# Two-layer decoder step, mixer: the beginning reordered, the turned rows of x kept in DRAM, the bias rows copied per pair of heads from SBUF

## The chip, the cores and the metric

The kernel runs on one core of one Trainium2 chip. The core has a matrix engine (TensorE, "PE" in the profile, with its weight loads as "PEld"), a vector engine (VectorE, "DVE"), a scalar engine (ScalarE, "ACT"), a general one (GpSimd, "POOL") and a small one that here only issues DMAs (SyncE, "SP"). DMAs are carried out by 16 DMA engines that all issuing engines share. The metric is the time of one execution in microseconds (us) on the device.

## The reference: what is computed

The program is one inference step of a hybrid decoder layer on 544 tokens, 512 of a prompt and 32 of a sample group (8 sequences of 4 tokens), with a model width of 1024. All numbers are fp32.

```
h = RMSNorm_pre(x)
[x_r | q | k | v | g] = h @ W_in
A: x_r -> causal conv of width 4 -> RG-LRU (gates, scan)
B: attention over a window of 128, 8 query heads, 2 key/value heads,
   a sink per head, a bias by relative position (rel_bias by bucket)
m = (sigmoid(g_A) * (A @ W_lru_o) + sigmoid(g_B) * (B @ W_attn_o)) @ W_out
x = x + RMSNorm_post(m)
u = RMSNorm_pre2(x) @ W_up ; causal conv of width 3
x = x + RMSNorm_post2((gelu(u_gate) * u_val) @ W_down)
```

The outputs are the new x of both groups, the states of the LRU and of both convolutions, and the key and value caches. In the bias, the score of query i and key j gets `rel_bias[bucket(i - j), head]`, and minus infinity outside the window.

## The kernel before, in words

**Products.** An fp32 product is made of three: each operand is split into a high part (fp32r) and the rest, and hi·hi, hi·lo and lo·hi are added up in PSUM. A weight block of 1024 x 128 (512 KB, a "key") is loaded by SP into one of five raw buffers (`wload`, L254) and split in two units of four 128x128 blocks: `wsplit_hi` on ACT (L277) and `wsplit_lo` on DVE (L282). One `step` (L331) multiplies a key with one half of the tokens (columns 0 to 255 or 256 to 543; in the later projections 272 and 272), which is 8 chunks x 3 = 24 matmuls into one PSUM tile (`pmin` for W_in, `pmlo` for W_lru_o, `pmout` for W_out).

**Order.** PE, ACT and DVE run exactly in the order of the program text. After each step a `tick` (L194) issues the other work: first the high splits of the weights that are claimed, two keys ahead, then whatever generators are due (`start_at(t, ...)` puts one on the list from tick t on; each `yield` ends its share of a tick), then the evacuations of the step before (`late`), then the low splits, and at the end what is in `last`. In the kernel before, the instructions of POOL and SP are put in order by the framework's planner, in the kernel after those of SP alone. An engine waits for semaphores in its own order: an instruction that waits holds up everything behind it on that engine. A DMA waits on the engine that issues it, and is then carried out by the DMA engines.

**The beginning.** SP loads x of the first two token blocks (four halves of 256 KB in all), a few norm rows, then weights and the rest of x. PE runs 36 matmuls on constants (WARM = 18 in the text, each of them two passes), then turns the 8 norm rows (`ps_rows_a`, L386). The mean square is taken on ACT and DVE, x is scaled by 1/rms (L423, L425), and PE turns x into 8 chunks of 128 channels x 256 tokens (`ps_ta`, L448). From each, ACT writes the high part of h, multiplied by the norm weight (`hH`, L433) and DVE the low part (`hL`). Then the first product runs: 8 hi·hi matmuls, 8 with the low weights, 8 with hL. In ticks 1 and 2 the same is done for the other 288 tokens (`norm_b`, `ps_tb` L461), for the steps from the fifth on.

**Bias tables.** `attn_tables` (L545 on) starts at tick 2. One matmul pair (`ps_ohp`) gives 8 rows (one per head) of 384 bias values by distance. DVE copies them to SBUF (`rvec`, L549), POOL stores them to DRAM (`rscr`, L550, 12 KB) and then repeats each row 128 times with one DMA from DRAM to DRAM (`rrep`, L553, 1536 KB). From `rrep` the table of a pair of heads, 128 x 2 x 256, is loaded with a row shift of one element per query (`btab`, L581), at ticks 5, 11, 18 and 27. The first softmax of a head pair adds it to the scores (`s` <- `psc`, `btab` on DVE, L177).

**Sample tables.** `sample_tables` starts at tick 12. POOL copies 16 small blocks of `rel4` into `lt` (L559), loads a one-hot matrix `ohs` (L561) and two masks `mk` (L565), and PE multiplies `ohs` and `lt` (`ps_bs`). The product stands in PE's order between two steps of W_in, so PE does nothing else until `ohs` and `lt` are there.

**x again.** At the product with W_lru_o (16 steps of `pmlo`) x is needed unscaled and turned, as `x1`, for the residual sum after W_out. `x_again` (L995) loads the five token blocks anew into the raw buffers (`xx`, L998), PE turns them (`pxx`, L1004, 40 transposes in 10 groups), and ACT and DVE copy them into `x1` (L1008). In the same stage POOL adds the gated halves (`gl`, L1019, one 128x272 per step) and issues the stores of the LRU states (L907 to L910).

## Time and profile before

| | before |
|---|---|
| median of 3 runs | 1002.67 us (1002.42 to 1002.88) |
| profiled execution: its time | 1003.73 us |
| profiled execution: its span | 1002.0 us |
| TensorE clock granted, mean | 0.997 |
| PE busy | 988.9 us (99%) |
| DVE busy | 732.0 us (73%) |
| ACT busy | 579.4 us (58%) |
| POOL busy | 151.0 us (15%) |
| DMA: mean over the span | 133 GB/s |

The profile is of one execution; times inside it are counted from the start of the span. In a row of the timeline stand the start, the duration, the engine, the line of the kernel, the operation, and the tile that is written <- the tiles that are read, then the number of instructions that were put together in the row; what stands in square brackets is the time that the engine was idle before it and what it waited for. An engine name with a q behind it is its instruction queue, which issues DMAs. In a row of the windows stand, for a stretch of time, the busy time of PE, PEld, DVE, ACT and POOL (with the number of instructions), the clock that TensorE was granted (1.00 is full), the busy share of the 16 DMA engines and the GB/s moved. In the list of DMA issues stand the number, the KB of each and the median time from the issue to the landing.

### The profile page before, as it was taken

How to read it: one execution, taken by the hardware profiler on the slowest of the kernel's cores; microseconds unless marked ns; L12 is line 12 of the kernel's file. 1: busy time of each engine (PE TensorE's matmuls, PEld its weight loads, DVE VectorE, ACT ScalarE, POOL GpSimd, SP SyncE). 2: the span in 40 equal slices, each digit the busy share in tenths (PEclk: the TensorE clock that was granted, in tenths of full speed). 3: DMA queues.
4: the chain of work that ended last, by engine and by line, in shares of the span. 5: the costliest groups of instructions: out<-in, count | busy, mean ns of one | idle time of the engine just before them, and what ended most of it. 6: DMA issues, size and time to landing. Idle time of an engine off the chain costs nothing.

```text
span 1002.0 us, 20195 instructions
## 1 busy us (share of the span) xinstructions
PE 988.9 (99%) x7837; PEld 978.5 (98%) x7837; DVE 732.0 (73%) x1555; ACT 579.4 (58%) x1422; POOL 151.0 (15%) x270
## 2 busy tenths in 40 slices
PE   8999999999999999999999999999999999999997
PEld 7999999999999999999999999999999999999996
DVE  6476687545846555589777788888888888887865
ACT  6444455469358535456776756565656565656652
POOL 3131010002304432110001111111111111110004
PEclk9999999999999999999999999999999999999999
DMA  7743223333322345327245858586867676767712
GB/s 211 231 150 93 64 77 105 99 91 94 102 68 85 106 138 148 105 66 210 71 116 124 193 124 192 125 191 127 189 133 184 139 177 145 171 160 167 216 45 90
DMA packets 207687, 133.40 MB, mean 133 GB/s; under 512 B 6546, under 2 KB 194306, under 8 KB 207560
## 3 DMA queue, kind: packets, MB, share of 16 engines
q1 hardware_dynamic: 197944, 112.20, 39.4%
q0 software_dynamic: 9600, 17.90, 11.3%
q10 hardware_dynamic: 48, 2.03, 0.5%
q8 instruction: 61, 1.00, 0.4%
q14 instruction: 34, 0.28, 0.1%
HBM read 111.82 MB, written 9.14 MB: 121 GB/s over the span
## 4 chain that ended last, share of the span: by engine, by line
PE 92%; DVE 3%; ACT 2%; DMA 2%; issue 0%; SPq 0%; ACTq 0%; DVEq 0%
PE pmin L165 22%; PE pmdn L165 16%; PE pux L1400 15%; PE puy L1400 7%; PE pq L1400 6%; PE pmout L165 5%; PE pmao L165 5%; PE pmlo L165 4%; PE puz L1400 4%; PE pg L165 1%; PE psc L165 1%; PE pvp L165 1%; DMA raw_up_s<-in_w_up_dram 1%; DMA raw_in<-in_w_in_dram 1%; PE pt L701 1%; PE ptok L165 1%
## 5 line engine op out<-in xcount | busy, mean ns | idle before, releaser
L165 PE MATMUL pmin<-hH,wh_in 128*128 128x256 f32 (+1 forms) x576 | 167.8, 294 | 0.0
L165 PE MATMUL pmin<-hH,wl_in 128*128 128x256 f32 (+1 forms) x576 | 164.7, 288 | 0.0
L165 PE MATMUL pmin<-hL,wh_in 128*128 128x256 f32 (+1 forms) x576 | 164.6, 288 | 0.0
L165 PE MATMUL pmdn<-fH,wh_dn 128*128 128x256 f32 (+1 forms) x448 | 129.2, 288 | 0.2 <-DVE ft L174 0.2
L165 PE MATMUL pmdn<-fH,wl_dn 128*128 128x256 f32 (+1 forms) x448 | 129.2, 288 | 0.2 <-DVE wl_dn L168 0.2
L165 PE MATMUL pmdn<-fL,wh_dn 128*128 128x256 f32 (+1 forms) x448 | 129.1, 288 | 0.0
L177 DVE SCALAR_TENSOR_TENSOR uc<-u,fv,uc 128x560 f32<-128x560 f32 x128 | 102.0, 797 | 13.3 <-ACT uc L1431 13.2
L165 PEld LDWEIGHTS pmin<-hH,wh_in 128*128 128x128 f32 x576 | 108.9, 190 | 1.9 <-issue 1.2
L165 PEld LDWEIGHTS pmin<-hL,wh_in 128*128 128x128 f32 x576 | 108.1, 188 | 0.0
L165 PEld LDWEIGHTS pmin<-hH,wl_in 128*128 128x128 f32 x576 | 107.9, 188 | 0.0
L165 PEld LDWEIGHTS pmdn<-fH,wh_dn 128*128 128x128 f32 x448 | 84.5, 189 | 0.6 <-issue 0.6
L165 PEld LDWEIGHTS pmdn<-fH,wl_dn 128*128 128x128 f32 x448 | 84.4, 188 | 0.4 <-DVE wl_dn L168 0.4
L165 PEld LDWEIGHTS pmdn<-fL,wh_dn 128*128 128x128 f32 x448 | 84.3, 188 | 0.0
L1526 ACT COPY u<-pux 128x272 f32<-128x272 f32 x52 | 20.1, 387 | 86.1 <-PE pux L1400 86.1
L168 DVE TENSOR_TENSOR u<-puy,u 128x240 f32<-128x240 f32 (+2 forms) x78 | 24.6, 344 | 49.8 <-PE puy L1400 32.1
L174 DVE TENSOR_TENSOR ft<-ft,pmdn 128x256 f32<-128x256 f32 (+1 forms) x104 | 45.2, 436 | 16.7 <-PE pmdn L165 16.1
L277 ACT ACTIVATE wh_in<-raw_in 128x512 fp32r<-128x512 f32 x72 | 44.2, 629 | 19.3 <-PE pmin L165 8.4
L282 DVE TENSOR_TENSOR wl_in<-raw_in,wh_in 128x512 fp32r<-128x512 f32 x72 | 48.2, 683 | 0.8 <-ACT wh_in L277 0.8
L1431 ACT ACTIVATE uc<-u,fv 128x560 f32<-128x560 f32 x64 | 48.2, 754 | 0.0
L664 ACT ACTIVATE s<-s,st 128x256 f32<-128x256 f32 (+1 forms) x32 | 15.2, 475 | 50.4 <-DVE st L661 43.0
L168 DVE TENSOR_TENSOR wl_dn<-raw_dn,wh_dn 128x512 fp32r<-128x512 f32 x56 | 38.3, 684 | 0.0
L1326 POOL DMA_DIRECT2D raw_up_s<-raw_up_s x26 | 22.7, 874 | 102.9 <-issue 5.2
(776 smaller groups left out, 3404.3 us busy)
## 6 DMA issues: line engine op xcount, KB each, us to landing
raw_in<-in_w_in_dram SPq DMA_DIRECT2D x36, 512.0 KB
raw_dn<-in_w_down_dram SPq DMA_DIRECT2D x56, 256.0 KB
raw_up_s<-in_w_up_dram SPq DMA_DIRECT2D x26, 512.0 KB
raw_up_s<-raw_up_s POOLq DMA_DIRECT2D x26, 256.0 KB, 5.9
raw_ao<-in_w_attn_o_dram SPq DMA_DIRECT2D x8, 512.0 KB
raw_lo<-in_w_lru_o_dram SPq DMA_DIRECT2D x8, 512.0 KB
raw_out<-in_w_out_dram SPq DMA_DIRECT2D x8, 512.0 KB
x1d<-x SPq DMA_DIRECT2D x8, 272.0 KB
```

Of the source, the lines that this page charges most:

```text
L165: pe.matmul(out, l, r, start=start, stop=stop)
L168: dve.tensor_tensor(out=out, in0=a, in1=b, op=ALU.subtract)
L174: dve.tensor_tensor(out=out, in0=a, in1=b, op=ALU.add)
L177: dve.scalar_tensor_tensor(out=out, in0=a, scalar=s_, in1=b, op0=op0, op1=op1)
L277: act.activation(hl[0], raw, AF.Copy)
L282: (eng or dve).tensor_tensor(out=hl[1], in0=raw, in1=f32(hl[0]), op=ALU.subtract)
L664: act.activation(s3[:, j, :], s3[:, j, :], AF.Exp, bias=ng[:, j:j + 1], accum_out=sm[:, j:j + 1])
L701: pe.transpose(pt[:, (2 * ch + j) * P:(2 * ch + j + 1) * P], s3[:, j, ch * P:(ch + 1) * P], ident)
L1326: pool.dma_start(out=w["p4"], in_=w["p2"], accum_op=ALU.add)
L1400: pe.matmul(ps[:, :HN], w, x, start=start and k == 0 and i == 0, stop=stop and k == 3 and i == 2, skip_group_check=True)
L1431: act.activation(yt[j][:, 0:FLATU], u[:, 0:FLATU], AF.Copy, scale=fv[:, j:j + 1])
L1526: act.copy(e[nm_], z)
```

## The change

The beginning of the mixer is written anew:

- Loads. The norm rows `rows_a` are loaded between the two first blocks of x. `relx`, `ohp`, the other norm rows and `rel4` are loaded on SP's queue, no longer on POOL's; the weights 3 and 4 come behind the first of them. 12 warming passes (24 matmuls) stand ahead of the turning of the norm rows and 11 (22 matmuls) behind it.
- First product. The low splits of the first key go to POOL. The transposes of two chunks share a PSUM tile (four tiles `ps_ta0` to `ps_ta3`), and the first product is spread between the transposes: the hi·hi and hi·lo matmuls of a chunk come as soon as its parts are written, the 8 with low weights at the end.
- The turned rows of x are kept: `keep_a` copies the 8 chunks of 256 tokens from PSUM to eight SBUF slots `xn` (four on ACT, four on DVE, at the ends of ticks 1 and 2), `keep_b` the 8 of 288 tokens. At tick 6 `put_away` takes the reciprocal of 1/rms and stores it and the 8 slots (272 KB each) to DRAM (`rmsd`, `xdram`).
- `x_again` loads the 8 chunks into `x1` and a row of rms repeated over all partitions, and POOL multiplies each chunk (128x544) by it, one per tick. No loads of `xx`, no transposes, no copies.
- Bias rows. `rvec` is no longer stored to DRAM and repeated with one DMA for all 8 rows. For each pair of heads `load_rep` issues one DMA on POOL that reads the pair's two rows of `rvec` in SBUF, each 128 times, and writes `rrep` of that pair (384 KB) to DRAM; `load_btab` then loads the table as before. The four copies are due at ticks 4, 5, 12 and 20, the tables at 4, 9, 17 and 26.
- POOL's instructions run in the order of the text too, with those of PE, ACT and DVE. In that order stand, after the first splits: copy 0, table 0, copy 1, table 1, the stores `kout` and `vout` of the first key/value head, copy 2, the 16 copies into `lt`, `ohs`, `mk`, the 23 small instructions of the gate constants (`lz` to `cc`), table 2, and later copy 3 and table 3.

```diff
@@ -72,7 +72,8 @@
 FIRST = 5
 ATTN = (8, 10, 12, 14, 16, 18, 20, 22, 24, 27, 30, 33, 36, 39, 42, 45)
 SAMPLE = (41, 46)
-WARM = 18
+WARM = 12
+KEEP = 11
 GATES = (51, 53, 55, 57, 73, 74, 75, 76)
 EXPS = (58, 59, 60, 61, 78, 79, 80, 81)
 SCANS = (62, 63, 65, 67, 82, 83, 85, 86)
@@ -138,7 +139,7 @@
     ctx.enter_context(tc.manual_schedule(engines={pe.engine}))
     mixer = ExitStack()
     cp = mixer.enter_context(tc.tile_pool(name="mixer_const", bufs=1))
-    mixer.enter_context(tc.manual_schedule(engines={act.engine, dve.engine}))
+    mixer.enter_context(tc.manual_schedule(engines={act.engine, dve.engine, pool.engine}))
 
     def S(name, dt=F32):
         return sp.tile([P, SLOT], dt, tag="s", name=name)
@@ -314,13 +315,6 @@
 
     def mmhalf(ps, key, X, a, ks=range(KD)):
         n = X.half[a][1] - X.half[a][0]
-        if key == order[0] and a == 0:
-
-            for j, (i0, i1) in enumerate(((0, 0), (1, 0), (0, 1))):
-                for k in ks:
-                    mm(ps[:, :n], wunits[2 * wpos[key] + k // 4][i0][:, k % 4, :], X.get(k, a, i1),
-                       j == 0 and k == 0, j == 2 and k == KD - 1)
-            return
         for k in ks:
             wh, wl = (wunits[2 * wpos[key] + k // 4][j][:, k % 4, :] for j in range(2))
             xh, xl = X.get(k, a, 0), X.get(k, a, 1)
@@ -330,9 +324,11 @@
 
     def step(key, X, a, done, target=None, look=2, quick=False):
 
-
-        ps = PM("pm" + "_".join(str(z) for z in key) + f"_{a}")
-        if quick:
+        first_ = key == order[0] and a == 0
+        ps = first_ps if first_ else PM("pm" + "_".join(str(z) for z in key) + f"_{a}")
+        if first_:
+            pass
+        elif quick:
             mmhalf(ps, key, X, a, range(4))
             now[0] += 0.5
             sides()
@@ -361,22 +357,23 @@
             nc.sync.dma_start(out=xt[i, z][:n, 0:512], in_=src[:, 512 * z:512 * z + 512])
 
     xload(0)
+    nc.sync.dma_start(out=rows_a[0:8, :], in_=I["norm_mix_pre"].rearrange("o (k p) -> (o k) p", p=P))
     xload(1)
-    nc.sync.dma_start(out=rows_a[0:8, :], in_=I["norm_mix_pre"].rearrange("o (k p) -> (o k) p", p=P))
     wload(0)
     wload(1)
     xload(2)
     xload(3)
     xload(4)
-    for i in (2, 3, 4):
-        wload(i)
+    wload(2)
     relx = cp.tile([NBK + 1, NH], F32, name="relx")
     pool.memset(relx, 1.0)
-    pool.dma_start(out=relx[0:NBK, :], in_=I["rel_bias"])
+    nc.sync.dma_start(out=relx[0:NBK, :], in_=I["rel_bias"])
     ohp = T("ohp")[:NBK + 1, 0:3 * WIN]
-    pool.dma_start(out=ohp, in_=I["c_ohp"])
+    nc.sync.dma_start(out=ohp, in_=I["c_ohp"])
     for r, nme in ((8, "norm_mix_post"), (16, "norm_ffn_pre"), (24, "norm_ffn_post")):
-        pool.dma_start(out=rows_a[r:r + 8, :], in_=I[nme].rearrange("o (k p) -> (o k) p", p=P))
+        nc.sync.dma_start(out=rows_a[r:r + 8, :], in_=I[nme].rearrange("o (k p) -> (o k) p", p=P))
+    wload(3)
+    wload(4)
     pv = keep.tile([P, 96], F32, name="pv")
 
     pw = PX("ps_warm")
@@ -384,6 +381,8 @@
     for z in range(WARM):
         mm(pw[:, (z % 4) * P:(z % 4 + 1) * P], ones, ident, True, True)
     pe.transpose(ps0[:, 0:8], rows_a[0:8, :], ident[0:8, 0:8])
+    for z in range(KEEP):
+        mm(pw[:, (z % 4) * P:(z % 4 + 1) * P], ones, ident, True, True)
     G_PRE, G_POST, G_FPRE, G_FPOST, C_W, C_B, C_BR, C_BI, C_LAM = 0, 8, 16, 24, 32, 64, 72, 80, 88
 
     def newton_rstd(r, v, s_, sq):
@@ -435,22 +434,63 @@
 
     xsquares(0)
     xsquares(1)
+    act.copy(pv[:, 0:8], ps0[:, 0:8])
     xrstd(0, 2)
-    split = [wsplit_hi(u) for u in wclaim(2)]
-    xscale(0, "av")
-    xscale(1, "vv")
-    dve.tensor_copy(pv[:, 0:8], ps0[:, 0:8])
-    for u in split:
-        wsplit_lo(*u)
+    u0, u1 = wclaim(2)
+
+    def scale0(i, z):
+        dve.tensor_scalar(xt[i, z][:, 0:512], xt[i, z][:, 0:512], ss[:, 1, i:i + 1], None, ALU.mult)
+
+    scale0(0, 0)
+    scale0(1, 0)
+    act.activation(xt[1, 1][:, 0:512], xt[1, 1][:, 0:512], AF.Copy, scale=ss[:, 1, 1:2])
+    scale0(0, 1)
+    first_ps = PM("pm_first")
+
+    def first_mm(k, i0, i1, start=False, stop=False):
+        mm(first_ps[:, :256], wunits[k // 4][i0][:, k % 4, :], h.get(k, 0, i1), start, stop)
+
+    ps_ta = []
+    wsplit_lo(*wsplit_hi(u0), eng=pool)
+    for k in range(KD + 3):
+        if k < KD:
+            if k % 2 == 0:
+                ps_ta.append(PX(f"ps_ta{k // 2}"))
+                for z in range(4):
+                    pe.transpose(ps_ta[-1][:, z * P:(z + 1) * P], xtile(z % 2, k + z // 2), ident)
+            hsplit(k, 0, ps_ta[-1][:, k % 2 * 256:k % 2 * 256 + 256])
+        if k == 1:
+            wsplit_lo(*wsplit_hi(u1), eng=pool)
+        if 0 <= k - 2 < KD:
+            first_mm(k - 2, 0, 0, start=k == 2)
+        if 0 <= k - 3 < KD:
+            first_mm(k - 3, 0, 1)
     for k in range(KD):
-        ps = (PM if k in (5, 6) else PX)(f"ps_ta{k}")
-        for i in range(2):
-            pe.transpose(ps[:, i * P:(i + 1) * P], xtile(i, k), ident)
-        hsplit(k, 0, ps[:, :256])
+        first_mm(k, 1, 0, stop=k == KD - 1)
+
+    xn = [S(f"xn{k}") for k in range(KD)]
+    xdram = drp.tile([KD, P, NT], F32, name="xdram")
+    rms = cp.tile([P, 5], F32, name="rms")
+    rmsd = drp.tile([5, P], F32, name="rmsd")
+
+    def keep_a(k):
+        (dve.tensor_copy if k % 2 else act.copy)(xn[k][:, 0:256], ps_ta[k // 2][:, k % 2 * 256:k % 2 * 256 + 256])
+
+    def keep_b(k, ps):
+        (act.copy if k % 2 else dve.tensor_copy)(xn[k][:, 256:NT], ps[:, :288])
+
+    def put_away():
+        dve.reciprocal(rms, ss[:, 1, :])
+        nc.sync.dma_start(out=rmsd.rearrange("i p -> p i"), in_=rms)
+        for k in range(KD):
+            nc.sync.dma_start(out=xdram[k], in_=xn[k][:, 0:NT])
+        yield
 
     def norm_b():
         last.extend(lambda i=i: xsquares(i) for i in (2, 3, 4))
-        yield
+        last.extend(lambda k=k: keep_a(k) for k in range(4))
+        yield
+        last.extend(lambda k=k: keep_a(k) for k in range(4, KD))
         last.append(lambda: xrstd(2, 5))
         last.extend(lambda i=i, e=e: xscale(i, e) for i, e in ((2, "av"), (3, "av"), (4, "vv")))
         yield
@@ -459,7 +499,7 @@
             for i in (2, 3, 4):
                 t0, n, _ = TOK[i]
                 pe.transpose(ps[:, t0 - 256:t0 - 256 + n], xtile(i, k), ident[:n, :n])
-            late.append(lambda k=k, ps=ps: hsplit(k, 1, ps[:, :288]))
+            late.append(lambda k=k, ps=ps: (hsplit(k, 1, ps[:, :288]), keep_b(k, ps)))
             if k in (3,):
                 yield
 
@@ -535,22 +575,17 @@
     pool.memset(lt, 0.0)
     rel4 = cp.tile([P, NH], F32, name="rel4")
     for t in range(DT):
-        pool.dma_start(out=rel4[32 * t:32 * t + 32, :], in_=I["rel_bias"])
+        nc.sync.dma_start(out=rel4[32 * t:32 * t + 32, :], in_=I["rel_bias"])
     biasS = cp.tile([P, 2, SKEY], F32, name="biasS")
-    rscr = drp.tile([NH, 3 * WIN], F32, name="rscr")
-    rrep = drp.tile([NH, P, 3 * WIN], F32, name="rrep")
+    rvec = cp.tile([NH, 3 * WIN], F32, name="rvec")
+    rrep = [drp.tile([2, P, 3 * WIN], F32, name=f"rrep{hp}") for hp in range(4)]
     btab = {}
 
     def attn_tables():
         ps = PX("ps_ohp")
         mm(ps[:NH, 0:3 * WIN], relx, ohp, True, True)
         yield
-        rvec = T("rvec")[:NH, 0:3 * WIN]
         dve.tensor_copy(rvec, ps[:NH, 0:3 * WIN])
-        pool.dma_start(out=rscr, in_=rvec)
-
-        a = rscr[:, :]
-        pool.dma_start(out=rrep, in_=bass.AP(a.tensor, a.offset, [[3 * WIN, NH], [0, P], [1, 3 * WIN]]))
         yield
 
     def sample_tables():
@@ -574,9 +609,13 @@
             add(biasS[:, g, :], ps[:, 0:SKEY], mk[g])
         yield
 
+    def load_rep(hp):
+        r = rvec[2 * hp:2 * hp + 2, :]
+        pool.dma_start(out=rrep[hp], in_=bass.AP(r.tensor, r.offset, [list(r.ap[0]), [0, P], [1, 3 * WIN]]))
+
     def load_btab(hp):
         bt = S(f"btab{hp}")[:, 0:512].rearrange("p (h j) -> p h j", h=2)
-        src = rrep[2 * hp:2 * hp + 2, :, :]
+        src = rrep[hp][:, :, :]
         a = bass.AP(src.tensor, src.offset + WIN - 1, [[3 * WIN - 1, P], [3 * WIN * P, 2], [1, 2 * WIN]])
         pool.dma_start(out=bt, in_=a)
         btab[hp] = bt
@@ -916,11 +955,13 @@
         yield
 
     start_at(1, norm_b())
+    start_at(6, put_away())
     start_at(2, attn_tables())
     start_at(9, params())
     start_at(14, cache_shift())
     for hp in range(4):
-        start_at((5, 11, 18, 27)[hp], once(load_btab, hp))
+        start_at((4, 5, 12, 20)[hp], once(load_rep, hp))
+        start_at((4, 9, 17, 26)[hp], once(load_btab, hp))
     start_at(12, sample_tables())
     for u, (hp, n) in enumerate((hp, n) for hp in range(4) for n in range(4)):
         start_at(ATTN[u], attn_unit(hp, n))
@@ -992,23 +1033,18 @@
 
     x1 = [S(f"x1_{k}") for k in range(KD)]
 
-    def x_again(i):
-        t0, n, src = TOK[i]
-        x_i = RAW(f"xx{i}")
-        nc.sync.dma_start(out=x_i[:n, :], in_=src)
-        yield 2 + i // 4
-        for kk in range(2):
-            px = PX(f"pxx{i}_{kk}")
-            for j in range(4):
-                k = 4 * kk + j
-                pe.transpose(px[:, j * P:j * P + n], x_i[:n, k * P:(k + 1) * P], ident[:n, :n])
+    def x_again():
+        full = T("rms_full")[:, 0:NT]
+        a = rmsd[:, :]
+        nc.sync.dma_start(out=full, in_=bass.AP(a.tensor, a.offset, [[0, P], [1, NT]]))
+        for k in range(KD):
+            nc.sync.dma_start(out=x1[k][:, 0:NT], in_=xdram[k])
+        yield 3
+        for k in range(KD):
+            pool.tensor_tensor(out=x1[k][:, 0:NT], in0=x1[k][:, 0:NT], in1=full, op=ALU.mult)
             yield
-            for j in range(4):
-                k = 4 * kk + j
-                (dve.tensor_copy if j % 2 else act.copy)(x1[k][:, t0:t0 + n], px[:, j * P:j * P + n])
-
-    for i in range(5):
-        start_at(now[0] + 3 + 2 * i, x_again(i))
+
+    start_at(now[0] + 3, x_again())
     M = Pairs("m")
 
     def lo_done(c):
```

## The prediction

> **What bounds the kernel now.** The page's busy times and its chain come first.
>
> ```profile
> PE 988.9 (99%) x7837; PEld 978.5 (98%) x7837; DVE 732.0 (73%) x1555; ACT 579.4 (58%) x1422; POOL 151.0 (15%) x270
> PE 92%; DVE 3%; ACT 2%; DMA 2%; issue 0%; SPq 0%; ACTq 0%; DVEq 0%
> ```
>
> PE is the bound. Time is won where PE's work is taken out or where PE waits, and lost where PE gets a new wait. Next, PE's waits:
>
> ```profile
> PE ps_ta L448 <- ACT x L423: 3.4, 1, 3.4
> PE ps_warm L165 <- POOL relx L374: 1.5, 1, 1.5
> PE pxx L1004 <- DMA xx<-in_x_prompt_dram: 0.9, 1, 0.9
> ```
>
> Two of the three lie where the change works. The sums below are made in the profiled execution (1003.73 us, span 1002.0) and then put on the median, 1002.67, which is 1.06 lower.
>
> **The W_lru_o stage: a gain.** The chain of this stage, in order of time (start, duration, what):
>
> ```profile
> 335.66 15.00 PE pmlo L165 x120
> 350.67 0.44 PE pxx L1004 x4
> 357.97 3.03 PE pmlo L165 x24
> 361.00 0.44 PE plr L904 x4
> 368.50 4.50 DMA xx<-in_x_prompt_dram
> 383.61 3.21 PE pmlo L165 x24
> 390.40 4.63 PE pmout L165 x37
> ```
>
> The 16 steps take 390.40 - 335.66 = 54.7 us. The pure steps are 16 x 3.0 (15.00 / 5) = 48.2, and the two `plr` groups stay, 0.9. So the ten `pxx` groups, the wait for `xx` and their slowing of neighbours cost at most 5.7; two steps of 3.21 may be slow for another reason (0.4). I take 5.3 off. What takes their place is off PE: 8 loads of 272 KB on SP, and 8 POOL multiplies of 128x544.
>
> ```profile
> L1019 POOL TENSOR_TENSOR gl<-gl,ga 128x272 f32<-128x272 f32 x16 | 17.5, 1092 | 37.5 <-DVE gl L171 27.7 <-ACT wh_lo L277 6.3 <-ACT wh_out L277 3.5
> L881 POOL TENSOR_TENSOR xc<-xc,lt 128x568 f32<-128x568 f32 x8 | 12.3, 1537 | 2.8 <-ACT lt L880 2.8
> ```
>
> A multiply costs about 1.5 us, an add 1.1; together 2.6 per tick of 3.0. POOL has room, if little, and PE needs the sums only at `pmout`. The removed 40 copies free ACT and DVE, which were not the bound.
>
> **The beginning: about nothing.** PE starts turning x at 11.07 and the first product ends at 17.32.
>
> ```profile
> 11.07 2.90 PE L448 MATMUL ps_ta<-ident,x 128*128 128x128 f32 x16 [3.43 <-ACT x L423]
> 17.32 0.28 PE L165 MATMUL pmin<-hH,wh_in 128*128 128x256 f32 x1
> 12.50:15.00 2.50, 2.50 (x13) 2.50 (x13) 2.50 (x8) 2.50 (x8) 1.63 (x12) 0.50 1.18 239
> ```
>
> The last row is of the windows: after the wait of 3.43, TensorE was granted half its clock. Interleaving lets the first product follow the splits, and two low splits leave DVE: by ACT's and DVE's rows I get an end near 16.3, a gain of 1.0. The bounds are 0 (the half clock falls worse) and 2.7 (with 1.7 of half clock saved by the KEEP passes). Against it stand the copies to `xn`:
>
> ```profile
> L1526 ACT COPY u<-pux 128x272 f32<-128x272 f32 x52 | 20.1, 387 | 86.1 <-PE pux L1400 86.1
> L788 DVE COPY spt<-pst 128x256 f32<-128x256 f32 x2 | 0.8, 417 | 0.0
> 20.27 0.16 DVE L174 TENSOR_TENSOR ss<-ss 128x3 f32<-128x3 f32 x1
> 23.25 0.54 DVE L549 COPY rvec<-ps_ohp 8x384 f32<-8x384 f32 x1
> 23.92 2.19 PE L461 MATMUL ps_tb<-ident,x 128*128 128x128 f32 x12
> ```
>
> Four copies on DVE (1.7 us) and four on ACT (1.5) come ahead of the second rms at 20.27, then the scaling, `rvec` at 23.25, and `ps_tb`, which PE reaches at 23.92 with almost no slack. So 1.7 later less 1.0 earlier: +0.7 for `rvec` and `ps_tb`, +0.5 for PE after it (range -1.2 to +1.3). `keep_b` adds 8 copies over six ticks, and `put_away` 8 stores of 272 KB on SP; both engines have idle time there, nothing taken. `ohp` and `relx` now queue behind a third weight on SP; `ps_ohp` was at 20.25, and I keep a bound of +1 for that.
>
> **The bias rows: a loss.** POOL's queue before:
>
> ```profile
> 24.09 0.52 POOL L550 DMA_DIRECT2D rscr<-rvec  x1 [9.88 <-DVE rvec L549]
> 28.27 1.11 POOL L553 DMA_DIRECT2D rrep<-rscr  x1 [3.67 <-DMA rscr<-rvec]
> 42.12 0.76 POOL L581 DMA_DIRECT2D btab<-rrep  x1 [12.73 <-DMA rrep<-rscr]
> 43.07 0.73 POOL L581 DMA_DIRECT2D btab<-rrep  x1
> 53.97 0.57 POOL L617 DMA_DIRECT2D out_dram<-kout  x1 [10.17 <-DVE kout L616]
> 54.76 0.56 POOL L641 DMA_DIRECT2D out_dram<-vout  x1 [0.22 <-DVE vout L640]
> 55.31 0.54 POOL L561 DMA_DIRECT2D ohs<-in_c_ohs_dram  x1
> 11.32 2.89 POOL L559 COPY lt<-rel 32x8 f32<-32x8 f32 x16 [4.66 <-DMA rel<-in_rel_bias_dram]
> ```
>
> and the landings of these DMAs, 24 to 70 us (last number, from the issue), and what needs them:
>
> ```profile
> rrep<-rscr POOLq DMA_DIRECT2D x1, 1536.0 KB, 13.6
> ohs<-in_c_ohs_dram POOLq DMA_DIRECT2D x1, 160.0 KB, 2.5
> out_dram<-kout POOLq DMA_DIRECT2D x1, 64.0 KB, 1.9
> 47.52 0.42 DVE L177 SCALAR_TENSOR_TENSOR s<-psc,btab 128x256 f32<-128x256 f32 x1 [5.66 <-DMA btab<-rrep]
> 67.23 0.70 PE L165 MATMUL ps_bs<-ohs,lt 128*128 128x320 f32 x2
> ```
>
> After, POOL's order is copy 0, table 0 (waits until copy 0 has landed), copy 1, table 1 (waits for copy 1), `kout`, `vout`, copy 2, `lt`, `ohs`. So two whole copies stand on POOL ahead of `ohs`, and a third ahead of it among the DMAs of the same queue. PE waits for `ohs` at 67.23. All hangs on how long 384 KB take from two rows of SBUF. Three rows of the windows (time, length, five busy times, clock, DMA share, GB/s):
>
> ```profile
> 36.00:40.00 4.00, 4.00 (x32) 4.00 (x31) 1.66 (x3) 2.62 (x7) 0.00 (x0) 1.00 0.52 205
> 997.00:999.00 2.00, 0.00 (x0) 0.00 (x0) 0.00 (x0) 0.34 (x1) 0.00 (x0) 0.84 1.03 385
> 999.97:1000.57 0.60, 0.00 (x0) 0.00 (x0) 0.00 (x0) 0.00 (x0) 0.00 (x0) 0.50 0.85 236
> ```
>
> While `rrep` was written alone, from 8 source rows, half of the 16 DMA engines were busy, 205 / 8 = 25.6 GB/s each: I read it as one engine per source row. Two source rows then give two engines. If each keeps 25.6, the 393,216 bytes stream in 7.7 us: the low end. The other two rows speak for less: at the end of the kernel, stores from 128 SBUF partitions ran at 385 GB/s, the last ones, from 32 partitions, at 236, 14.75 per engine, with all engines at it. Engines that read few neighbouring partitions were slowed by each other. Two engines on two neighbouring rows at 14.75 each need 13.3 us; sharing one engine's 25.6 they need 15.4. I take the middle, 14.3, since this is the nearest case (few SBUF rows as the source), and keep 7.7 to 15.4. Around the stream, `rrep` spent 13.6 - 9.6 (1536 KB at 164 GB/s, half of the engines shared at first) = 4.0, the small DMAs 1.9 to 2.5: I take 4.0 for copy 0, which meets the weight loads, and 2.2 for the others.
>
> [...]
>
> The sum on POOL: copy 0 issued at 24.09 + 0.7 = 24.8, landed 24.8 + 18.3 = 43.1; table 0 issued, +0.8 = 43.9; copy 1 landed 43.9 + 16.5 = 60.4; table 1, `kout`, `vout` issued, 0.73 + 0.57 + 0.56 = 62.3; copy 2 landed 62.3 + 16.5 = 78.8. `ohs` is issued near 65.7 (0.5 for the copy, 2.9 for `lt`), but its share on copy 2's engines stands behind it, so it lands about 79.0. PE stands from 67.2 (the 0.5 from the beginning goes into this wait) to 79.0: +11.8. After such a wait half the clock for 3.4 us, as at 12 to 15 us: +1.7. Table 0 lands 5.4 us after its issue (42.12 to 47.52 before), at 48.5, where DVE wanted it at 47.5: hidden by the later wait. Tables 2 and 3 are 20 us and more ahead of their use.
>
> Sum: -5.3 + 11.8 + 1.7 = +8.2. That is 1011.9 on the profiled execution and **1010.9** on the median.
>
> **The rivals.**
>
> *The copies run fast enough (faster).* With two engines at 25.6 each, copy 0 lands at 36.5, copy 1 at 47.2; `kout` then waits for its data as before, copy 2 goes out at 55.3 and lands at 65.2, `ohs` with it: no stall. The sum is -5.3 + 0.5, **997.9**. For it speaks `rrep`'s 25.6 per row; against it, that `rrep` read from DRAM. The point of decision: `ohs` lands at 36.1 + 3s with s the stream of one copy, so the loss eats the gain when 3s + 36.1 - 67.2 + 1.7 = 5.3, s = 11.6 us, or 34 GB/s for both rows together.
>
> *`ohs` isn't held by copy 2 (faster).* Then it lands at 65.7 + 2.5 = 68.2, a stall of 1.0, and the time is 1002.67 - 5.3 + 1.0 to 2.7, **998.4 to 1000.1**. Against it, weakly, the landings of the tables issued at 42.12 and 43.07:
>
> ```profile
> btab<-rrep POOLq DMA_DIRECT2D x1, 256.0 KB, 5.3
> btab<-rrep POOLq DMA_DIRECT2D x1, 256.0 KB, 6.2
> ```
>
> The first was done at 47.4, the second 1.9 later: in order, not shared evenly. [...]
>
> *Worse.* At 15.4 and 4.0 around each copy, `ohs` lands at 24.8 + 58.2 + 2.6 + 0.3 = 85.9: +18.7, with 1.7 to 3.4 of half clock, **1018 to 1019**. POOL falling behind in the W_lru_o stage would add to it: 0.4 us short per tick, should multiplies cost 1.9, is 3 us, most of it before `pmout` needs it.
>
> **How the numbers follow.** Stall of 8 to 16 us (1007 to 1015): 0.58. The worse case: 0.10. Copies fast: 0.20; `ohs` not held: 0.08; a stall near the gain: 0.04. The last is the bound of what can be told, 0.2%, or 2 us. The range must hold 8 in 10 and has cases of both signs: 997 to 1018; the likeliest case alone, 1007 to 1015. Faster 0.29, same 0.04, slower 0.67.
>
> **What would show it.** A wait of PE at `ps_bs` for `ohs`; landings of about 17 us for the four copies in the list of DMA issues; DMA share near 0.13 while a copy runs alone; POOL idle before tables 0 and 1 for 15 us and more; clock 0.50 after the wait; `pmlo` from first to `pmout` in 49.4 us. It is wrong if a copy lands in under 12 us, if `ps_bs` follows without a gap, or if PE waits elsewhere, at `psc` for table 0 or at `ps_ohp`.

## The result, and the profile after

| | before | after |
|---|---|---|
| median | 1002.67 us (5 runs, 1002.29 to 1003.15) | 1035.41 us (5 runs, 1034.79 to 1036.22) |
| profiled execution: time, span | 1003.73, 1002.0 us | 1035.43, 1033.5 us |
| TensorE clock granted, mean | 0.997 | 0.983 |

The ratio is 1.0326, with a 95% interval of 1.0311 to 1.0341: 32.7 us slower, where 8.2 were forecast. The forecast had the direction and the place; the size was off by a factor of four, outside its range of 997 to 1018.

Busy times and chain of the changed kernel's page:

```profile
PE 990.5 (96%) x7807; PEld 977.4 (95%) x7807; DVE 733.0 (71%) x1541; ACT 578.0 (56%) x1411; POOL 163.3 (16%) x273
PE 84%; DMA 8%; DVE 4%; ACT 2%; issue 1%; POOL 1%; SPq 0%; ACTq 0%; DVEq 0%; POOLq 0%
```

PE's busy time is only 1.6 us above that of before, so nearly all of the loss is waiting, and the chain has 8% of DMA in it, where it had 2%. PE's waits name the places:

```profile
PE ps_bs L166 <- DMA ohs<-in_c_ohs_dram: 27.4, 1, 27.4
PE pux L1436 <- DVE wl_s_p L169: 3.0, 2, 2.9
PE pm_first L166 <- ACT hH L432: 2.1, 5, 0.6
PE ps_tb L501 <- ACT x L422: 0.7, 2, 0.4
```

The first is the forecast's wait, 27.4 us instead of 11.8. POOL's DMAs up to there (start, duration, what; in brackets the idle time before it and its cause; `kout`, `vout` and POOL's other work left out):

```profile
27.06 1.28 POOL L614 DMA_DIRECT2D rrep<-rvec  x1 [13.49 <-DVE rvec L588]
46.57 0.79 POOL L620 DMA_DIRECT2D btab<-rrep  x1 [18.23 <-DMA rrep<-rvec]
47.35 1.12 POOL L614 DMA_DIRECT2D rrep<-rvec  x1
72.58 0.75 POOL L620 DMA_DIRECT2D btab<-rrep  x1 [23.89 <-DMA rrep<-rvec]
74.44 1.11 POOL L614 DMA_DIRECT2D rrep<-rvec  x1
77.85 0.57 POOL L596 DMA_DIRECT2D ohs<-in_c_ohs_dram  x1
```

and the landings, 20 to 150 us:

```profile
rrep<-rvec POOLq DMA_DIRECT2D x4, 384.0 KB, 22.2
ohs<-in_c_ohs_dram POOLq DMA_DIRECT2D x1, 160.0 KB, 20.7
```

POOL stood 18 and 24 us ahead of the two tables. Then `ohs`, which landed 2.5 us after its issue before, took 20.7 behind copy 2, until 98.5. Two windows, one while copy 2 runs almost alone and one after PE's restart at 98.65:

```profile
90.00:95.00 5.00, 0.00 (x0) 0.00 (x0) 0.00 (x0) 0.00 (x0) 0.00 (x0) 0.50 0.12 25
98.65:104.00 5.35, 5.35 (x20) 4.47 (x21) 2.59 (x8) 0.00 (x0) 0.41 (x1) 0.50 0.40 109
```

The share of 0.12 is that of about two of the 16 engines, which move 25 GB/s together; and PE works the first 5.35 us after the wait at half its clock (from 104.50 to 105.00 the clock is 1.00 again).

Where the time came in, by the start of the same PE work in both timelines (after less before):

| PE reaches | later by, us | what lies between |
|---|---|---|
| first score product `psc` | 2.6 | the beginning |
| third `psc` | 3.8 | PE waits 0.8 for `qL` |
| `ps_bs` | 31.4 | the wait for `ohs` |
| sixth `psc` | 34.0 | half clock |
| `pmlo` | 33.8 | nothing |
| `pmout` | 27.9 | the W_lru_o stage, 5.9 shorter |
| `pux`, 90th group | 27.5 | nothing |
| the last matmul's end | 31.5 | the wait for `wl_s_p` at 955 us, and half clock after it |

The W_lru_o stage in the chain:

```profile
369.50 23.97 PE pmlo L166 x192
393.90 3.01 PE pmlo L166 x24
397.34 20.98 PE pmlo L166 x168
```

No transposes, no wait; POOL's multiplies were in time.

### The profile page after: what moved, and what is told of

Same layout as the page of the kernel before. It is cut to its first block, busy times and chain, and to the rows that moved or that the text cites. A ratio compares the mean times of both kernels' runs of the same rounds, so it can differ in the third digit from the quotient of the medians.

```text
span 1033.5 us, 20163 instructions
## 1 busy us (share of the span) xinstructions
PE 990.5 (96%) x7807; PEld 977.4 (95%) x7807; DVE 733.0 (71%) x1541; ACT 578.0 (56%) x1411; POOL 163.3 (16%) x273
## 4 chain that ended last, share of the span: by engine, by line
PE 84%; DMA 8%; DVE 4%; ACT 2%; issue 1%; POOL 1%; SPq 0%; ACTq 0%; DVEq 0%; POOLq 0%
PE pmin L166 17%; PE pmdn L166 16%; PE pux L1436 14%; PE puy L1436 7%; PE pq L1436 6%; PE pmout L166 5%; PE pmao L166 5%; PE pmlo L166 5%; DMA rrep<-rvec 4%; PE puz L1436 3%; DMA ohs<-in_c_ohs_dram 2%; DMA raw_up_s<-in_w_up_dram 2%; PE pg L166 1%; PE psc L166 1%; PE pvp L166 1%
## 5 line engine op out<-in xcount | busy, mean ns | idle before, releaser
L278 ACT ACTIVATE wh_in<-raw_in 128x512 fp32r<-128x512 f32 x72 | 44.3, 628 | 17.5 <-PE pmin L166 7.1
## 6 DMA issues: line engine op xcount, KB each, us to landing
xdram<-xn SPq DMA_DIRECT2D x8, 272.0 KB, 18.3
```

What stands on the lines that cost most here:

```text
L278: act.activation(hl[0], raw, AF.Copy)
```

## The experiments

All times stand beside runs of the kernel before on the same chip. In the short diffs the changed kernel is the base unless another is named.

**The bias rows by way of DRAM.**

```diff
-    load_rep(hp): rrep[hp] <- rvec rows 2hp, 2hp+1 in SBUF, x128
+    rscr <- rvec ; rrep (8 heads) <- rscr, x128, one DMA
```

> Edit: the bias rows go the way of the kernel before (rvec to DRAM, one copy of 1536 KB from DRAM to DRAM for all eight heads); everything else is the changed kernel. Theory (the four copies from SBUF hold POOL and, through their queue, ohs; the rest of the change is worth its own sum): the wait of PE at ps_bs goes from 27.4 us to under 1, the half clock after it goes too, and the time is the changed kernel's 1035.4 less 27.4 less about 2.6 of half clock, 1005.4, or down to 1001.7 if the 2.9 us wait for wl_s_p near the end (with its half clock, 3.7 in all) was a passing one. Rival (the reordering of POOL by hand costs by itself): PE still waits at ps_bs for 5 us and more, and the time stays above 1008.

Measured: 1017.2 us against 1003.6, ratio 1.0136 (1.0119 to 1.0153). The wait at `ps_bs` was gone, as the theory had it, but a new one stood earlier:

```profile
PE psc L166 <- DVE s L178: 9.1, 1, 9.1
rrep<-rscr POOLq DMA_DIRECT2D x1, 1536.0 KB, 20.0
rmsd<-rms SPq DMA_DIRECT2D x1, 2.5 KB, 20.2
```

The copy from DRAM took 20.0 us, not 13.6 as before, so table 0 was late for the second `psc`, with half clock behind it (0.50 from 64.8 to 68.0 us). Neither expectation had that, and the time is 12 us above the 1005.4 expected. Something else of the change slows POOL's DMAs.

**`ohs` ahead of the copies.**

```diff
+    start_at(3, sample_loads())    # lt, ohs, mk, ahead of load_rep(0)
-    (the same lines at tick 12)
```

> Edit: the 16 copies into lt and the loads of ohs and the masks stand ahead of the first copy of bias rows on POOL; the four copies from SBUF stay. Theory (only the queueing of ohs behind two copies on POOL and a third among the DMAs hurts; the copies themselves have room): PE's wait at ps_bs is gone, the copies still take 19 to 25 us to land, table 1 lands near 80 where its first softmax wants it near 90, and the time is within 2 us of the run with the copy from DRAM. Rival (the copies are too slow in any order): PE waits for table 1, 2 or 3 at a later score product, by 5 us or more, and the time is above 1010.

Measured: 1024.6 us, ratio 1.0211 (1.0184 to 1.0238). The rival, one table earlier than it said: PE waited for table 0 instead.

```profile
PE psc L166 <- DVE s L178: 11.9, 1, 11.9
PE pkn L781 <- POOL vn L696: 3.0, 1, 3.0
```

The copies into `lt` had to wait for `rel4`, copy 0 went out at 31.2 and table 0 only at 61.1. With copies this slow, whatever stands behind them on POOL is late; the second row is POOL's small copy `vn`, held behind a table.

**The rows apart.**

```diff
-    rvec rows of heads in partitions 0..7
+    rvec rows of heads in partitions 0, 16, 32, ...
```

> Edit: the eight bias rows stand 16 partitions apart in SBUF (heads in partitions 0, 16, 32 and so on) instead of in partitions 0 to 7; the copies, their order and their size are unchanged. Theory (two neighbouring partitions share one way out of SBUF of about 26 GB/s, so that two DMA engines take turns): packets of 4608 bytes go from 360 to 180 ns each, the stream of a copy from 14.5 to about 7.7 us, the landing of a copy from 22 to 11 to 15 us, ohs lands near 63 to 70 instead of 98.5, PE waits 0 to 3 us at ps_bs, and the time is 1001 to 1008. Rival (two DMA engines reading SBUF with a repeated row are slow wherever the rows stand): landings stay at 19 to 25 us and the time at 1035.

Measured: 1026.8 us, ratio 1.0229 (1.0214 to 1.0244). Landings, and a window while copy 2 ran:

```profile
rrep<-rvec POOLq DMA_DIRECT2D x4, 384.0 KB, 17.4
83.00:88.00 5.00, 0.00 (x0) 0.00 (x0) 0.00 (x0) 0.00 (x0) 0.00 (x0) 0.50 0.14 56
```

The rate is the theory's: about the same share of the engines as in the changed kernel (0.14, 0.12) moves 56 GB/s instead of 25. A DMA is carried out in packets, whose times and bytes the trace keeps: those of 4608 bytes took 178 ns each here (the median), where the median was 360 to 380 in three of the changed kernel's four copies. The landings are not the theory's: 17.4 us, since only 8 us of copy 2 are its stream. Most of its packets came after 80.7, 13 us after the issue; before that, the two copies of the caches (992 KB each) sent packets of 63 KB, most of which took 2.3 to 2.9 us each. So the loss against the kernel before fell only from 32.7 to 23.2 us, and the 1001 to 1008 expected were missed.

**One copy of eight rows straight from SBUF.**

```diff
-    four copies of 2 rows x 128
+    rrep (8 heads) <- rvec rows 0..7 in SBUF, x128, one DMA
```

> Edit: one copy of all eight rows straight from SBUF (1536 KB) takes the place of the four copies of two rows; no row is stored to DRAM first. The rows stand in partitions 0 to 7. Theory (four neighbouring partitions share one way out of about 26 GB/s, so eight rows have two of them): the stream takes 1536 KB / 52 GB/s = 30 us, the landing 34 us, table 0 is issued near 61 and DVE's first softmax waits for it, so PE waits 12 us or so at the second score product. Rival (each source row has an engine of its own at 25.6 GB/s, as in the copy from DRAM): the landing is 12 to 14 us, as with the copy from DRAM, and PE doesn't wait.

Measured: 1025.9 us, one run. The landing, and a window while the copy ran almost alone:

```profile
rrep<-rvec POOLq DMA_DIRECT2D x1, 1536.0 KB, 35.9
56.00:62.00 6.00, 1.46 (x12) 1.22 (x10) 0.00 (x0) 0.00 (x0) 0.00 (x0) 1.00 0.51 66
```

This is the disputed cost by itself. The row of before with the copy from DRAM has 205 GB/s at a share of 0.52; here a share of 0.51 moves 66. Not all of that is the copy: by the packets of 4608 bytes its own part is 184 of the 205 before, 48 of the 66 here, 22 of the 25 in the changed kernel and 46 of the 56 with the rows apart. The 35.9 us stand against 34 forecast by two ways out of SBUF and 12 to 14 by an engine per row. That four neighbouring rows share one way out was the author's assumption: the run shows 48 GB/s for eight rows, about twice the 22 of two, and not which rows share. PE waited 16.8 us for table 0.

**The stores of the kept rows later, in the text.** Two runs: on the kernel with the copy from DRAM, and on the changed kernel.

```diff
-    start_at(6, put_away())
+    start_at(30, put_away())
```

> Edit: as the run with the copy from DRAM, and the stores of the kept rows (eight of 272 KB and the scattered rms row) go out at tick 30 instead of tick 6. Theory (these stores share the DMA engines with the bias rows: in the run with the copy from DRAM the 12 KB store took 5.8 us to land against 3.9 before and the copy of 1536 KB 20.0 against 13.6, so that table 0 came 9.1 us too late for the second score product): the copy lands in 13 to 15 us, PE doesn't wait at the second score product and isn't put on half clock there, and the time falls by 9.1 + 3.4, from 1017.2 to 1004.6, or to 1001 if the wait for wl_s_p near the end goes too. Rival (the copy is slowed by the weight loads that now run beside it, since it starts 5 us later than before): the landing stays near 20, and so does the wait.

Measured: 1007.1 us against 1003.2, ratio 1.0036 (1.0022 to 1.005).

```profile
rrep<-rscr POOLq DMA_DIRECT2D x1, 1536.0 KB, 13.1
PE pux L1436 <- DVE wl_s_p L169: 2.9, 1, 2.9
```

The landing was as forecast, and PE's wait at the second `psc` was gone; the time fell by 10.0 us, where 12.5 were expected. But the edit did less than it says: SP, which the planner orders, sent the eight large stores at 31 to 42 us all the same. Only the rms row moved, to 133 us, because it waits for a reciprocal on DVE, whose order is that of the text. That row is one DMA of 640 scattered numbers of 4 bytes. In the run without this edit, packets of the copy and of the weight loads took up to 3.6 us each from 44 to 50 us, right behind it. With the row at 133 us no such packets stood beside the copy, and the large stores went out at the same time as without the edit. So the 7 us came from the small scattered store and not from the 2.2 MB.

> Edit: the changed kernel, with the same stores moved from tick 6 to tick 30 and nothing else. Theory (the second copy took 24.7 us instead of 17 because of these stores, 8 us of the loss): copy 1 lands in 17 to 18 us, ohs lands near 89 to 91 instead of 98.5, PE waits 18 to 20 us at ps_bs, and the time is 1025 to 1028. Rival (the second copy is slow for another reason, say the weight loads): landings of 19, 25 and 22 us as before, and 1035.

Measured: 1035.6 us, ratio 1.0323 (1.0308 to 1.0339): no change, the rival. Copy 1 landed 23.4 us after its issue, 24.7 in the changed kernel. Here too only the rms row had moved, so it cost copy 1 about 1.3 us, and the run leaves the large stores open.

**The beginning alone.** As with the copy from DRAM, and x read again as before, nothing kept.

```diff
-    keep_a, keep_b, put_away, x_again from xdram
+    x_again of the kernel before
```

> Edit: as the run with the copy from DRAM, but x is read again, turned and copied in the W_lru_o stage as before, and nothing of it is kept; so the reordered beginning is left, with POOL by hand. Theory (the copies of kept rows on ACT and DVE cost the beginning 1.5 to 2 us, the pairing of two chunks in one PSUM tile another 2): PE reaches the first score product 0.3 to 1.0 us later than before (2.7 later with the copies), the W_lru_o stage takes its 54.7 us again, and the time is within 1 us of the kernel before, or 3 to 4 above it if the wait for wl_s_p near the end stands here too. Rival (the copies had cover and cost nothing): PE is 2.6 us later as in the changed kernel.

Measured: 1005.7 us against 1003.2, ratio 1.002 (1.001 to 1.0029). PE reached the first `psc` 2.6 us later than before, as in the changed kernel, though without the copies: the rival, so far. But the start differs: here PE waited 1.7 us for x at its first chunk and was granted 0.59 of its clock from 10 to 17.5 us, against 1.00 in the changed kernel's profile. From `ps_ohp` (+2.6) to `psc` (+2.6) nothing was added, where the changed kernel adds 1.9 (+0.7 to +2.6): that is what the copies cost. The other traces agree: between these two points PE takes 23.4 to 23.5 us in the six kernels of this document without the copies, 25.1 to 25.3 in nine of the ten with them and 26.1 in the tenth. When x arrives varies more: in the twelve kernels with the norm rows between the blocks of x, PE starts turning x between 9.0 and 10.6 us. So the 2.6 us to the first `psc` is one trace's number; the other traces of kernels with these copies and pairs have 2.7 to 4.6.

**A PSUM tile per chunk.** On the beginning alone.

```diff
-    ps_ta0..3, two chunks of 256 in each
+    ps_ta0..7, one chunk in each
```

> Edit: as the run with the beginning alone, but each turned chunk has a PSUM tile of its own, as in the kernel before, instead of two sharing one. Theory (in the changed kernel ACT's high part of the odd chunk waited about 0.55 us for DVE's low part of the even chunk, four times, because both read one tile): these four waits go, the first product ends about 2 us earlier (16 instead of 18), and PE reaches the first score product 1 to 2 us earlier than in the run with the pairs. Rival (the first product is bound by the alternation of ACT and DVE in any case): no gain from it, within 0.3 us.

Measured: 1002.8 us, ratio 0.9993 (0.9984 to 1.0002). PE reached the first `psc` at 44.15 instead of 46.25, 2.1 us earlier. ACT's high parts in the changed kernel, then in this run:

```profile
12.99 0.84 ACT L432 ACTIVATE hH<-ps_ta,pv 128x256 fp32r<-128x256 f32 x2 [0.55 <-DVE hL L178]
```

```profile
12.36 0.84 ACT L432 ACTIVATE hH<-ps_ta,pv 128x256 fp32r<-128x256 f32 x2
```

In the trace of the changed kernel, four of ACT's high parts of an odd chunk stand 0.55 to 0.58 us idle until DVE's low part (`hL`) of the even chunk of the same tile is done. With a tile each, none of them waits for DVE.

**The stores really late, then the caches too, then the rows apart.** The stores are issued by ACT, whose order is that of the text.

```diff
-    nc.sync.dma_start(...)   in put_away, tick 6
+    act.dma_start(...)       in put_away, tick 30
```

> Edit: the changed kernel, with the stores of the kept rows and of the rms row issued by ACT at tick 30, so that they really leave the first 100 us (in the run with the stores moved in the text alone, SP issued the eight large ones at 31 to 52 us all the same; only the rms row moved). Theory (the second copy is slowed by these stores, which read the same SBUF partitions and share the engines): copy 1 lands in 17 to 18 us instead of 24, ohs near 91, PE waits 18 to 21 us at ps_bs, time 1026 to 1029. Rival (the weight loads slow it): copy 1 stays at 22 us and more, time above 1032.

Measured: 1043.9 us, ratio 1.0404 (1.0386 to 1.0421), slower than the changed kernel. The edit brought a wait of its own:

```profile
161.55 12.23 ACTq L486 DMA_DIRECT2D xdram<-xn  x8
173.82 0.38 ACT L860 ACTIVATE xr<-pmin 128x256 f32<-128x256 f32 x1 [13.61 <-DMA xdram<-xn]
```

ACT spent 12.2 us on issuing eight stores, and PE waited 7.3 us for ACT, 9.5 with the half clock behind it. Leaving that aside: copy 1 landed 21.1 us after its issue, 3.6 less than in the changed kernel. Of these 3.6 the run above gives 1.3 to the rms row, so the large stores cost copy 1 about 2.3; the 17 to 18 us expected were not reached.

```diff
     (as above, and)
-    start_at(14, cache_shift())
+    start_at(36, cache_shift())
```

> Edit: as the run with the stores issued late, and the two copies of the caches from DRAM to DRAM (992 KB each, packets of 63 KB) go out at tick 36 instead of 14. Theory (the first packet of copy 2 came 7 us after its issue, not 2 to 3, because the packets of the cache copies, 2.4 to 2.9 us each, stand between): copy 2 lands in 17 to 18 us instead of 22 to 24, ohs lands 5 to 6 us earlier than with the caches at tick 14, time lower by as much. Rival (copy 2 starts late because POOL writes its packets' addresses late): no change.

Measured: 1038.8 us, ratio 1.0355 (1.0339 to 1.037), 5.1 us less than with the caches early. The wait at `ps_bs` went from 25.8 to 20.7, `ohs` landed 17.0 us after its issue instead of 22.0. With nothing large beside them, the copies still landed in 19.1 to 20.8 us. For copy 1 these are 3.5 us from the issue to the first packet, 16.2 of stream (371 ns for a packet of 4608 bytes, two at a time) and 0.4 to the landing.

```diff
     (as above, and)
+    rvec rows in partitions 0, 16, 32, ...
```

> Edit: as the run with stores and cache copies late, and the bias rows 16 partitions apart. Theory: each copy streams in 8 us and lands in 10 to 12, copy 2 goes out when kout and vout are ready, near 60, and ohs lands near 70 to 72, within 2 us of PE's reaching it at 71 to 72: PE waits 0 to 2 us at ps_bs, and the time is 1004 to 1008, as in the run with the copy from DRAM and the rms row late (1007.1), the beginning and the wait near the end being what is left. Rival (POOL's order costs in any case): PE waits 5 us and more.

Measured: 1015.1 us, ratio 1.0116 (1.0101 to 1.0131). The first lines of PE's waits, and the copies:

```profile
PE pmin L166 <- ACT xr L860: 6.0, 1, 6.0
PE pux L1436 <- DVE wl_s_p L169: 2.8, 1, 2.8
rrep<-rvec POOLq DMA_DIRECT2D x4, 384.0 KB, 12.5
```

No wait at `ps_bs` any more; PE reaches it 3.8 us later than before, which is what the beginning cost. The partitions alone (the run before against this one) take 23.7 us off. What is left over the forecast is the edit's own wait on ACT: 6.0 and its half clock, 7.8 together. Without it the time would be an estimated 1007.3.

**x first.** On the beginning with a PSUM tile per chunk.

```diff
-    xload(0); rows_a; xload(1)
+    xload(0); xload(1); rows_a
```

> Edit: as the run with the beginning alone and a PSUM tile per chunk, and the norm rows are loaded behind the first two blocks of x, as in the kernel before, not between them. Theory (the rows' load, 0.4 us of SP's issue and eight small rows, delays the second block, on which the scaling waits: PE waited 1.6 us for it at the first turned chunk): PE starts turning x 0.3 to 0.5 us earlier, time 1002.3 to 1002.6 against 1002.8, a little below the kernel before. Rival (the first rows of x arrive when the DMA engines, which are full, let them): no difference.

Measured: 1001.9 us against 1003.2, ratio 0.9987 (0.9977 to 0.9996): 1.2 us less than the kernel before. PE starts turning x at 9.64 (11.07 before, 10.29 with the rows between) and reaches the first `psc` 1.4 us earlier than before:

```profile
9.64 0.85 PE L459 MATMUL ps_ta<-ident,x 128*128 128x128 f32 x6
14.87 1.10 PE L166 MATMUL pm_first<-hH,wl_in 128*128 128x256 f32 x8
```

So the beginning without the pairs and with x first is worth 1.2 us. How much of it is the load order isn't shown: the two medians, 1002.8 and 1001.9, come from two chips, and their intervals against the kernel before overlap. In the traces, PE waits 0.2 to 1.8 us for x at the first turned chunk in nine of the twelve kernels with the rows between, and in none of the three with x first; but these three start turning x at 9.6 to 10.4 us, which is no earlier.

**The wait near the end.** It stood in all ten kernels that keep the rows in DRAM (the changed one and nine of the runs), 2.5 to 3.0 us of `pux` waiting for `wl_s_p`, 3.0 to 4.1 from the 90th to the last `pux` group with the half clock where it follows (in the changed kernel 0.50 from 957.65 to 961.05 us), and in none of those that read x again (the kernel before and the runs of the beginning alone). The instructions of that part are the same in both. On DVE, `wl_s_p` stands behind a sum that waits for a weight load (start, time to the landing; the changed kernel, then the kernel before):

```profile
946.89 8.41 DMA raw_up_s<-in_w_up_dram
917.04 7.29 DMA raw_up_s<-in_w_up_dram
```

SP sends this load 29.9 us later than before, while PE is 27.5 later, and it takes 1.1 longer. Why it leaves late is the question of the next two runs.

```diff
     (x first, and)
+    two unused DRAM tiles as large as the kept rows and the rms row
```

> Edit: the beginning alone with a PSUM tile per chunk and x first, plus two unused tiles in DRAM of the sizes of the kept rows and the rms row, so that the scratch that is allocated behind them (the x of the second half, the rows of u) lies where it lies in the changed kernel; 288 numbers are written into them, nothing is read. Theory A (the wait of PE for wl_s_p near the end, 2.5 to 3.0 us in all kernels that keep rows and absent in all that don't, comes from where the DRAM scratch lies): it appears here. Theory B (it comes from which SBUF slots the late tiles get) or C (from the traffic or the times of the kept rows themselves): it doesn't.

Measured: 1002.4 us, one run; no such wait.

```diff
     (x first, and)
+    eight slots of the SBUF ring taken where the kept rows take them
```

> Edit: the same kernel with eight slots of the SBUF ring allocated where the changed kernel takes them for the kept rows, one column of each set to zero on POOL and nothing else done with them, so that the later tiles rotate through the same slots as in the changed kernel. Theory B: the wait for wl_s_p near the end appears, 2.5 to 3.0 us. Theories A and C: it doesn't; POOL's eight small writes cost nothing on PE's path.

Measured: 1002.0 us, one run; no such wait. Neither place makes it by itself. Of theory C, the time of the stores isn't it either: with the stores issued by ACT from 161.6 us on, the wait still stood (2.6 us). What does make it stays open; no run tests the traffic of the kept rows alone.

## Why the prediction was right or wrong, point by point

- *The bias rows: a loss.* Right in the mechanism: POOL's order, `ohs` late behind copy 2 (20.7 us), PE's wait at `ps_bs`. The runs with the copy from DRAM, and with the rows apart and the other traffic late, take that wait away. The size was off. The sum had `ohs` at 79.0, it came at 98.5, and the 19.6 us are these: copy 0 went out at 27.1, not 24.8 (2.3); it took 19.2, not 18.3 (0.9); copy 1 took 24.7, not 16.5 (8.2); copy 2 and `ohs` behind it 24.1 after copy 2's issue, not 16.7 (7.4); issues between them 0.8.
- *"2.2 for the others", around a stream of 14.3.* This is the step that failed: the landing of copies 1 and 2, put at 16.5. Copy 1 took 24.7. With the rms row late it took 23.4, with the large stores late too 21.1, with the caches late as well 20.1. Of the 8.2 us that the forecast lacked here, 4.6 are the traffic beside the copy, 3.6 of that the stores of the kept rows, which it priced as "nothing taken". The other 3.6 are the copy's own: 16.2 of stream, not 14.3, and 3.9 around it, not 2.2, a figure read from small DMAs. For `ohs` behind copy 2 the cache copies cost 5.0, and the forecast had no term for them.
- *Two engines on two neighbouring rows share.* Right: 25 GB/s for both in the changed kernel, 56 with the rows 16 partitions apart, 66 (48 of them the copy's) at a share of 0.51 for eight rows in partitions 0 to 7 against 205 (184) from DRAM. By what way the rows share isn't shown.
- *Half the clock after the wait, 1.7.* It was 2.6: the clock stayed at 0.50 for at least the first 5.35 us of work, longer than the 3.4 us taken from the beginning of the kernel before (0.50 from 11.93 to 15.34). What ends the half clock isn't shown: behind the 2.9 us wait near the end of the changed kernel it was 3.4 us again (957.65 to 961.05); at `ps_bs` the clock had been at 0.50 since 73.6, 2.4 us into the wait, and was so until 104.3.
- *The beginning: about nothing.* Wrong in sign for its first half: the first product ended near 18, not 16.3. The step that failed is the reading of ACT's and DVE's rows, in which they follow each other freely; the shared PSUM tiles made them alternate (ACT idle 0.55 to 0.58 us, four times). The copies cost what was said (1.9, with 1.7 on DVE forecast). With the KEEP passes in place, the clock went with PE's wait for x: from 10 to 17.5 us it was 1.00 in the changed kernel, where PE didn't wait for x, and 0.59 to 0.64 in the six paired kernels where it waited 1.3 to 1.8 us. No run leaves the passes out, so their own share isn't shown.
- *The W_lru_o stage, 5.3 off.* Right: 5.9.
- *The rivals.* "The copies run fast enough" rested on 25.6 GB/s for each engine, which the copy from DRAM gave (205 at a share of 0.52) and two neighbouring rows didn't (25 for both). "`ohs` isn't held": fell, 20.7 us against 2.5. That its share stands behind copy 2's on the same engines was the author's assumption in the sum; no run shows the order on an engine, only the landings: behind copy 2 20.7 us, 17.0 with stores and caches late, 8.9 with the rows apart as well, and 6.2 where `ohs` stood ahead of the copies. "Worse" had the mechanism at 18.7 of delay and was still short.
- *What no step had:* 4.1 us near the end, behind a weight load that left late; why it did was not found.

The loss by the starts of PE's work: 2.6 in the beginning, 1.2 to the third `psc`, 27.6 at `ps_bs`, 2.6 of half clock, -0.2 up to `pmlo`, -5.9 in the W_lru_o stage, -0.5 up to the 90th `pux`, and 4.1 after it. The sum is 31.5, as between the ends of PE's last matmuls; the profiled executions differ by 31.7, the medians by 32.7.

## What to carry to other kernels

Price a DMA by where its rows lie, not by its bytes alone: two neighbouring SBUF rows repeated 128 times ran at 25 GB/s, two rows 16 partitions apart at 56; eight neighbouring rows ran at 66, eight rows from DRAM at 205. On an engine that runs in text order, a wait for a DMA's landing holds every later issue (POOL stood 18 and 24 us ahead of two tables), so put what PE needs first ahead of it, and look up what the queue already holds at that time (`ohs` took 20.7 us behind copy 2, 2.5 before). When two engines read one PSUM tile by turns, look whether the program makes them wait for each other (0.55 to 0.58 us here, four times).

## What the runs showed that was not expected

- A store of 640 numbers of 4 bytes to scattered places, sent while a copy and weight loads ran, was followed by about 6 us in which their packets took up to 3.6 us each; moved to a quieter time, the copy of 1536 KB landed in 13.1 us instead of 20.0. In the changed kernel the same store, issued at 50.3 us, was followed by packets of up to 4.4 us from 58 to 63 us.
- Two copies between places in DRAM, with packets of 63 KB that mostly took 2.3 to 2.9 us each, made `ohs` on another queue land 5 us later (22.0 us after its issue against 17.0). By what way isn't shown; the trace doesn't tell the engine of a packet.
- Eight stores of 272 KB issued by ACT kept ACT from computing for 12.2 us, 1.5 us each.
- A wait of 2.5 to 3.0 us near the end went with the kept rows, 550 us earlier, in ten kernels of ten. Neither where the scratch lies nor which slots are taken makes it by itself.
